# A gathered prefix sum and product: the last list chunk in a place of its own, merged front transfers, reordered transposes, four product groups

## The chip, the cores and the metric

The kernel runs on one core of one Trainium2 chip. The metric is the device time of one launch in microseconds: the median over runs of the same kernel, and for a comparison the two kernels are run in turn on one chip.

## The reference

```python
def reference(x, lengths, w):        # x 8 x 8192 x 512 f32, lengths 8, w 512 x 512 f32
    pos = np.arange(S)[None, :, None]
    mask = (pos < lengths[:, None, None]).astype(np.float32)
    cs = np.cumsum(x * mask, axis=1)
    midpoints = (lengths // 2).clip(0)
    mid_features = cs[np.arange(B), midpoints, :]
    return np.matmul(mid_features[:, None, :], w).squeeze(1)
```

Only one row of each running sum is used: the sum of the first `lengths // 2 + 1` rows of a batch. So the kernel sums those rows, batch by batch, and multiplies the eight sums by w. How many rows that is depends on the data in `lengths`. For the drawn lengths (1138, 5379, 511, 4113, 1809, 7542, 7716, 1140) some 31 MB have to be read.

## The kernel before

**Reading the rows.** A unit is U = 8 consecutive rows of one batch (16 KB). A chunk is 128 units, one on each partition (2 MB). There are three kinds of reads.

- The front: the first 256 rows of every batch are read blind, before the lengths are known, as two chunks into slots 0 and 1 of a ring `xt` of R = 4 slots. SP issues them (L149 to L153): chunk 0 (batches 0 to 3) as four transfers, each to every fourth partition; chunk 1 (batches 4 to 7) as one transfer to all partitions.
- The list: the units beyond the front that the lengths ask for are numbered through over all batches. DVE works out for every partition and chunk the unit's number (`idx`, mark "idx") and the 0/1 weights (`wc`, mark "w"). GpSimd (POOL) issues one indirect transfer a chunk (`gather(c)`, L234). Here the list has 1520 units, 11.875 chunks, so 12 gathers; units beyond the list are skipped by the bounds check. A gather waits until its slot is free: the first two for ACT's zeroing of slots 2 and 3 (`s_zero`, L185; skipped units must leave finite data), the others for PE's `s_done` of the chunk that held the slot.
- The back: rows 256 to 511 of batches 0 and 1 are again read blind, into `xb` (two transfers, 0.5 MB each). They and w (`wt`, one transfer for its first half and two for its quarters) stand at the end of POOL's queue (`gp_tail`, L251), behind the last gather.

**Summing.** PE multiplies each chunk's rows by its weights: 8 products of 128x8 by 128x512, in f32 with two passes each, spread over four groups of 32 output partitions (`add`, L395, with `u % 4`), so s_ps holds four partial sums of 8 rows each. Weights of a chunk go into the ring `wr`: ACT copies them from `wc` when a slot is free (`weigh`, L197). SP relays to PE that the weights and data of a chunk are there (`relay`, L167; semaphore `s_rdy`). Ahead of each chunk but the first, PE runs two filler products (`idle`, L418) that wait for nothing. SP, ACT and PE run their chunks in loops over the four slots (`ring`, L137) with a count in a register, since the number of chunks is data.

**The tail.** After the last chunk PE (block `pe_end`) multiplies the back piece of batch 0 (`back(0)`, L444) into c_ps, then (block `pe_last`) that of batch 1. DVE copies s_ps to s_sb in two halves once `s_done` has counted all chunks (L378). PE then folds and transposes: four products with s_sb's quarters as weights (L462) and one with c_sb (L465) give mf_ps, the sums with the feature dimension on the partitions. DVE copies it to mf_sb. Then w: for each of four k, two products of 128x8 by 128x256 into two groups of 64 output partitions (L469 to L475), with a wait for wt's piece at k = 0, 2, 3. DVE copies one half of the output from o_ps, ACT the other, and SP and ACT each store a half (8 KB).

**The order of work** is written out by hand, engine by engine; nothing schedules it. DVE's steps count up `s_dve`, and `marks` names the counts that others wait for. A DVE step waits for the one before unless it says `wait=False`. Each DMA queue takes its transfers in the order of issue: SP's holds the front, POOL's all gathers, xb and wt.

Of the kernel before, what the change touches and what calls it, by code (L numbers as in the profile page):

```python
# [15 lines left out]
def kernel(  # L16
# [30 lines left out]
    FAR = 1 << 17  # L47
    IDLE = 2
    xu = x.rearrange("b (q u) d -> (b q) (u d)", u=U)
    lens_words = lengths.tensor.reshape([B]).bitcast(I32).ap().rearrange("(o t) -> o t", o=1)  # L50

# [8 lines left out]
    def sem(name):  # L60
        return tc.alloc_semaphore(name)

    xt = sb("xt", [P, R, U * D])
    xb = sb("xb", [P, BB, BU * D])
    wt = sb("wt", [P, KC, D])
# [32 lines left out]
    ge = sb("ge", [P, C, B + 1])  # L98
    idx = sb("idx", [P, C], I32)
    early = sb("early", [P, C, U, B])  # L100
    wc = sb("wc", [P, C, U * B])
    wr = sb("wr", [P, R * U * B])
    wb = sb("wb", [P, BB, BU, BB])
    fold_i = sb("fold_i", [P, B], I32)
# [17 lines left out]
    s_full = [sem(f"full{k}") for k in range(R)]  # L122
    s_front = [sem(f"front{k}") for k in range(FRONT)]
    s_back = [sem(f"back{k}") for k in range(BB)]
    s_w = [sem(f"w{k}") for k in range(3)]
    s_len, s_out, s_pool, s_dve, s_pe, s_done, s_wr, s_rdy, s_zero, s_act = (
        sem(n) for n in ("len", "out", "pool", "dve", "pe", "done", "wr", "rdy", "zero", "act"))

# [19 lines left out]
    def sync(sp):  # L148
        for b in range(FB):  # L149
            sp.dma_start(out=xt[b::FB, 0], in_=x[b, :HEAD].rearrange("(q u) d -> q (u d)", u=U),  # L150
                         ).then_inc(s_front[0], 16)
        sp.dma_start(out=xt[:, 1], in_=x[FB:, :HEAD].rearrange("b (q u) d -> q b (u d)", u=U),
                     ).then_inc(s_front[1], 16)  # L153
        left = sp.alloc_register("left_sp")
        full = sp.alloc_register("full_sp")
        have = sp.alloc_register("have_sp")
        sp.reg_mov(full, 16)
        sp.reg_mov(have, 1)
        sp.wait_ge(s_dve, marks["chunks"])
        sp.load(left, chunks[:])  # L160
        sp.wait_ge(s_dve, marks["front"])
        for f in range(FRONT):
            sp.wait_ge(s_front[f], 16 if f else 16 * FB)
            sp.sem_inc(s_rdy, 1)
        sp.br(f"sy_0_{FRONT}")

        def relay(s):  # L167
            sp.wait_ge(s_wr, have)
            sp.wait_ge(s_full[s], full)
            sp.sem_inc(s_rdy, 1)  # L170
            sp.reg_add(have, have, 1)
            if s == FRONT - 1:
                sp.reg_add(full, full, 16)

        ring(sp, "sy", left, relay)
        with nc.body("sy_end", valid_engines=[sp.engine]):
            sp.wait_ge(s_dve, marks["out"])
            store(sp, 0)
            sp.wait_ge(s_out, 32)
            sp.br(END)  # L180


    def scalar(act):
        act.dma_start(out=lens[:], in_=lens_words).then_inc(s_len, 16)
        for s in range(FRONT, R):  # L185
            act.memzero(xt[:, s]).then_inc(s_zero, 1)  # L186
        left = act.alloc_register("left_act")
        free = act.alloc_register("free_act")
        act.wait_ge(s_dve, marks["w"])
        act.load(left, chunks[:])  # L190
        for s in range(FRONT, R):
            act.copy(out=weights_of(s), in_=wc[:, s - FRONT]).then_inc(s_wr, 1)  # L192
        act.reg_sub(left, left, R)
        act.reg_mov(free, 1)
        act.br("ac_0_0")

        def weigh(s):  # L197
            act.wait_ge(s_done, free)
            col = act.snap(free)
            act.copy(out=weights_of(s),  # L200
                     in_=wc[:, bass.ds(col + (R - FRONT - 1), 1)].rearrange("p c e -> p (c e)"),
                     ).then_inc(s_wr, 1)
            act.reg_add(free, free, 1)

        ring(act, "ac", left, weigh)
        with nc.body("ac_end", valid_engines=[act.engine]):
            act.wait_ge(s_pe, 5)
            act.copy(out=o_sb[64:64 + B], in_=o_ps[64:64 + B, :D // 2]).then_inc(s_act, 1)  # L208
            act.wait_ge(s_act, 1)
            store(act, 1)  # L210
            act.br(END)
# [5 lines left out]
    def gpsimd(pool):  # L217
        pool.iota(p_i[:], pattern=[[0, 1]], base=0, channel_multiplier=1).then_inc(s_pool, 1)
        pool.wait_ge(s_pool, 1)
        for k in range(4):  # L220
# [11 lines left out]
                  ).then_inc(s_pool, 1)  # L232

        def gather(c):  # L234
            s = (c + FRONT) % R
            if c < R - FRONT:
                pool.wait_ge(s_zero, c + 1)
            else:
                pool.wait_ge(s_done, c + FRONT - R + 1)
            pool.indirect_dma_start(  # L240
                out=xt[:, s], out_offset=None, in_=xu,
                in_offset=bass.IndirectOffsetOnAxis(ap=idx[:, c:c + 1], axis=0),
                bounds_check=B * UB - 1, oob_is_err=False,
            ).then_inc(s_full[s], 16)

        n = pool.alloc_register("n_pool")
        pool.wait_ge(s_dve, marks["idx"])
        gather(0)
        pool.load(n, count[:])
        pool.br("gp_1")  # L250
        with nc.body("gp_tail", valid_engines=[pool.engine]):  # L251
            for b in range(BB):
                pool.dma_start(out=xb[:, b], in_=x[b, BACK].rearrange("(q u) d -> q (u d)", u=BU),  # L253
                               ).then_inc(s_back[b], 16)
# [5 lines left out]
            pool.br(END)  # L260
        for c in range(1, C):
            with nc.body(f"gp_{c}", valid_engines=[pool.engine]):
                pool.br_cmp(n, c, f"gp_go{c}", "gp_tail", "IS_GT")  # L263
            with nc.body(f"gp_go{c}", valid_engines=[pool.engine]):
                gather(c)
                pool.br(f"gp_{c + 1}" if c + 1 < C else "gp_tail")

# [4 lines left out]
    def vector(dve):  # L272
# [48 lines left out]
        step(ts, out=count[:], in0=up_i[:], scalar1=7, scalar2=None, op0=ALU.logical_shift_right)  # L321
        step(ts, out=chunks[:], in0=count[:], scalar1=float(FRONT), scalar2=None, op0=ALU.add)
        mark("chunks")
# [29 lines left out]
        for f in range(FRONT):  # L353
# [10 lines left out]
             in1=ge[:, :, :B].unsqueeze(2).to_broadcast((P, C, U, B)), op=ALU.mult)  # L364
        mark("w")
        fill(pick[:], 0)
        fill(wb[:], 0)
# [7 lines left out]
        mark("back")  # L375
        left = dve.alloc_register("left_dve")
        dve.load(left, chunks[:])
        dve.wait_ge(s_done, left)  # L378
        for at in HALVES:
            step(dve.tensor_copy, out=s_sb[:, at], in_=s_ps[:, at])  # L380
        mark("s")
        dve.wait_ge(s_pe, 3)
        step(dve.tensor_copy, out=c_sb[:], in_=c_ps[:, :P])
        mark("c")
        dve.wait_ge(s_pe, 4)
        step(dve.tensor_copy, out=mf_sb[:].rearrange("p k m -> p (k m)"), in_=mf_ps[:])
        mark("mf")
        dve.wait_ge(s_pe, 5)
        step(dve.tensor_copy, out=o_sb[:B], in_=o_ps[:B, :D // 2])
        mark("out")  # L390
# [3 lines left out]
    def tensor(pe):  # L394
# [9 lines left out]
        with nc.body("pe_main", valid_engines=[pe.engine]):  # L404
            pe.reg_mov(begin, 0)
            pe.wait_ge(s_dve, marks["ones"])
            for to, width in ((s_ps, D), (o_ps, D // 2), (c_ps, P), (mf_ps, KC * B)):
                pe.matmul(to[:, :width], lhsT=zero[:, :P], rhs=zero[:, :width], start=True, stop=False,  # L408
                          skip_group_check=True)
# [8 lines left out]
        def idle():  # L418
            for _ in range(IDLE):
                pe.matmul(idle_ps[:FB], lhsT=v_f[:, 0], rhs=rank[:].to_broadcast((P, D)),  # L420
                          start=True, stop=True, skip_group_check=True)

        def chunk(s):
            pe.sem_inc(s_rdy, -1)._wait_ge(s_rdy, 1)  # L424
            for u in range(U):
                mm = add(s_ps, u % 4, weights_of(s)[:, u * B:(u + 1) * B],
                         xt[:, s, u * D:(u + 1) * D])
            mm.then_inc(s_done, 1)

# [11 lines left out]
        with nc.body("pe_end", valid_engines=[pe.engine]):  # L441
            pe.wait_ge(s_dve, marks["back"])

            def back(b):  # L444
# [12 lines left out]
        with nc.body("pe_last", valid_engines=[pe.engine]):  # L457
            back(1)
            for k, at in enumerate(QUARTERS):
                if k in (0, 2):  # L460
                    pe.wait_ge(s_dve, marks["s"] - 1 + k // 2)
                pe.matmul(mf_ps[:, B * k:B * (k + 1)], lhsT=s_sb[:, at], rhs=fold[:], start=False,  # L462
                          stop=False, skip_group_check=True)
# [5 lines left out]
            for k in range(KC):  # L469
                if k in W_AT:  # L470
                    pe.wait_ge(s_w[W_AT.index(k)], 16)
                for g, cols in enumerate(HALVES):
                    mm = pe.matmul(o_ps[64 * g:64 * g + B, :D // 2], lhsT=mf_sb[:, k],  # L473
                                   rhs=wt[:, k, cols], start=False, stop=(k == KC - 1),
                                   skip_group_check=True, tile_position=(0, 64 * g))  # L475
            mm.then_inc(s_pe, 1)
# [39 lines left out]
```

## Time and profile before

| | us |
|---|---|
| median of 14 runs (84.19 to 85.42) | 84.86 |
| the profiled execution | 84.48 |
| its span, first to last instruction | 82.7 |
| first bytes of the front in the trace | 2.2 |
| first chunk on PE, start | 10.03 |
| a list chunk, start to start (63.55 to 68.44) | 4.89 |
| last chunk's products on PE | 72.76 to 74.66 |
| landing of the second back piece | 75.16 |
| products with w on PE | 77.39 to 79.31 |

Busy time in the span: PE 59.9, of which 25.6 are filler, weight loads 16.2, DVE 13.5, ACT 11.6, POOL 16.8. The 16 DMA engines moved 31.25 MB: 27.00 MB on the queue of POOL, 4.20 MB on that of SP. The granted TensorE clock is 1.00 throughout. From the issue of a gather to its landing the median is 16.6 us; 18.0 to 18.4 us for wt.

How to read it: a group's line gives the source line, engine, operation, tiles with their shapes, the count and the busy time. PE's records come in pairs, PEld (weight load) and PE (the product), and an f32 product has two of each. All DVE steps have the line of a helper, L276, so they are told apart by their tiles; so do most products (L396). An end of a product is modelled. In a table of stretches each row gives the busy time of each engine in it, the clock, the DMA engines' mean busy share and the rate. Times are from the span's start.

### The profile page before, as it was taken

To read this page: it belongs to the slowest core of one execution; us is meant where nothing else is said; L and a number is where in the kernel's file an instruction comes from. 1 tells how busy PE (TensorE), PEld (TensorE's weight loads), DVE (VectorE), ACT (ScalarE), POOL (GpSimd) and SP (SyncE) were. 2 spreads that over 40 slices of the span, in tenths; PEclk is the share of its full clock that TensorE was granted. 3 is DMA by queue.
4 is the path that set the end of the run, shared out by engine and by line. 5 is a ranking of instruction groups with operands and counts; after the bars stand their busy time and mean duration, and the time that the engine had idled before them with its cause. 6 is when DMAs were issued, how large, how long until landed. Compare 5 with 4: busy or idle time off the path is not lost. (4 is left out here: it accounts for less than half of the span.)

```text
span 82.7 us, 1040 instructions
## 1 busy us (share of the span) xinstructions
PE 59.9 (72%) x346; PEld 16.2 (20%) x346; DVE 13.5 (16%) x55; ACT 11.6 (14%) x16; POOL 16.8 (20%) x33
## 2 busy tenths in 40 slices
PE   0980499999959498593958949396693948889830
PEld 0470211123112020110202112020211102026500
DVE  4718899600000000000000000000000000005010
ACT  2999700300101001010000101001000000000010
POOL 4400540504120404022040401307900000000000
PEclk9999999999999999999999999999999999999999
DMA  0999999999999999999999999999999999999000
GB/s 0 357 333 365 396 444 404 436 436 404 452 412 452 436 404 452 412 452 436 396 460 412 436 444 396 452 428 420 444 400 436 452 396 444 373 410 392 34 3 4
DMA packets 2693, 31.25 MB, mean 378 GB/s; under 512 B 386, under 2 KB 402, under 8 KB 914
## 3 DMA queue, kind: packets, MB, share of 16 engines
q0 software_dynamic: 2320, 27.00, 77.1%
q1 hardware_dynamic: 352, 4.20, 13.3%
q8 instruction: 1, 0.02, 0.1%
q14 instruction: 2, 0.02, 0.0%
q10 hardware_dynamic: 18, 0.01, 0.0%
HBM read 31.46 MB, written 0.02 MB: 381 GB/s over the span
## 5 line engine op out<-in xcount | busy, mean ns | idle before, releaser
L396 PE MATMUL s_ps<-xt,wr 128*8 128x512 f32 x224 | 29.1, 625 | 14.8 <-PEq L424 14.8
L420 PE MATMUL idle_ps<-rank,v_f 128*4 128x512 f32 x52 | 25.6, 615 | 0.0
L240 POOL DMA_INDIRECT xt<-in_x_dram,idx x12 | 12.2, 1020 | 42.0 <-PE s_ps L396 35.6
L396 PEld LDWEIGHTS s_ps<-xt,wr 128*8 128x8 f32 x224 | 5.7, 90 | 35.6 <-issue 35.5
L276 DVE COPY s_sb<-s_ps 128x256 f32<-128x256 f32 x2 | 0.8, 424 | 58.8 <-PE s_ps L396 58.7
L420 PEld LDWEIGHTS idle_ps<-rank,v_f 128*4 128x4 f32 x52 | 4.7, 90 | 19.0 <-issue 19.0
L200 ACT COPY wr<-wc 128x64 f32 x10 | 2.4, 244 | 38.1 <-PE s_ps L396 37.8
L186 ACT ACTIVATE xt<-xt 128x4096 uint32<-128x4096 uint32 x2 | 7.1, 3608 | 0.0
L208 ACT COPY o_sb<-o_ps 8x256 f32<-8x256 f32 x1 | 0.4, 362 | 23.1 <-PE o_ps L473 23.1
L408 PE MATMUL s_ps<-zero 1*128 1x512 f32 x2 | 2.0, 1122 | 1.9 <-DVE row L276 1.9
L412 PE MATMUL b_ps<-row,ones 1*128 1x16 f32 x2 | 0.6, 380 | 2.3 <-DVE row L276 2.3
L276 DVE TENSOR_TENSOR wc<-early,ge 128x1984 f32<-128x1984 f32 x1 | 2.2, 2224 | 0.0
L276 DVE TENSOR_TENSOR early<-v,b_ps 128x1984 f32<-128x1984 f32 x1 | 2.2, 2222 | 0.0
L473 PE MATMUL o_ps<-wt,mf_sb 128*8 128x256 f32 x16 | 1.9, 379 | 0.3 <-DVE mf_sb L276 0.3
L186 ACT ACT_TABLE_LOAD x1 | 1.3, 1283 | 1.5 <-SPq L52 1.5
L396 PE MATMUL c_ps<-xb,wb 128*2 128x128 f32 x32 | 1.3, 276 | 0.1
L253 POOL DMA_DIRECT2D xb<-in_x_dram x2 | 1.2, 594 | 0.0
L192 ACT COPY wr<-wc 128x64 f32<-128x64 f32 x2 | 0.4, 242 | 5.4 <-DVE wb L276 5.4
L258 POOL DMA_DIRECT2D wt<-in_w_dram x2 | 1.1, 594 | 0.0
L462 PE MATMUL mf_ps<-fold,s_sb 128*128 128x8 f32 x8 | 1.1, 262 | 0.0
L408 PE MATMUL o_ps<-zero 1*128 1x256 f32 x2 | 1.1, 629 | 0.0
L462 PEld LDWEIGHTS mf_ps<-fold,s_sb 128*128 128x128 f32 x8 | 1.0, 194 | 0.2 <-DVE s_sb L276 0.2
(67 smaller groups left out, 18.8 us busy)
## 6 DMA issues: line engine op xcount, KB each, us to landing
xt<-in_x_dram SPq DMA_DIRECT2D x4, 512.0 KB
xt<-in_x_dram SPq DMA_DIRECT2D x1, 2048.0 KB, 11.0
xb<-in_x_dram POOLq DMA_DIRECT2D x2, 512.0 KB, 16.9
wt<-in_w_dram POOLq DMA_DIRECT2D x1, 512.0 KB, 18.0
wt<-in_w_dram POOLq DMA_DIRECT2D x2, 256.0 KB, 18.3
xt<-in_x_dram,idx POOLq DMA_INDIRECT x12, 16.6
lens<-in_lengths_dram ACTq DMA_DIRECT2D x1, 0.1 KB
out_dram<-o_sb ACTq DMA_DIRECT2D x1, 8.0 KB
```

What stands on the lines that cost most here:

```text
L186: act.memzero(xt[:, s]).then_inc(s_zero, 1)
L200: act.copy(out=weights_of(s), in_=wc[:, bass.ds(col + (R - FRONT - 1), 1)].rearrange("p c e -> p (c e)"),).then_inc(s_wr, 1)
L240: pool.indirect_dma_start(out=xt[:, s], out_offset=None, in_=xu, in_offset=bass.IndirectOffsetOnAxis(ap=idx[:, c:c + 1], axis=0), bounds_c ...
L253: pool.dma_start(out=xb[:, b], in_=x[b, BACK].rearrange("(q u) d -> q (u d)", u=BU),).then_inc(s_back[b], 16)
L258: pool.dma_start(out=wt[:, k], in_=w[QUARTERS[k]]).then_inc(s_w[k - 1], 16)
L276: do(*args, **kw).then_inc(s_dve, 1)
L396: return pe.matmul(to[32 * j:32 * j + weights.shape[1], :rows.shape[1]], lhsT=weights, rhs=rows, start=False, stop=False, skip_group_check ...
L408: pe.matmul(to[:, :width], lhsT=zero[:, :P], rhs=zero[:, :width], start=True, stop=False, skip_group_check=True)
L412: pe.matmul(to[:, :of.shape[1]], lhsT=ones[:], rhs=of[:], start=True, stop=True,).then_inc(s_pe, 1)
L420: pe.matmul(idle_ps[:FB], lhsT=v_f[:, 0], rhs=rank[:].to_broadcast((P, D)), start=True, stop=True, skip_group_check=True)
L462: pe.matmul(mf_ps[:, B * k:B * (k + 1)], lhsT=s_sb[:, at], rhs=fold[:], start=False, stop=False, skip_group_check=True)
L473: mm = pe.matmul(o_ps[64 * g:64 * g + B, :D // 2], lhsT=mf_sb[:, k], rhs=wt[:, k, cols], start=False, stop=(k == KC - 1), skip_group_check ...
```

## The change

- **Front.** SP issues each front chunk as one transfer, chunk 0 in the form of chunk 1: partition 4q + b holds unit q of batch b.
- **Last list chunk.** The ring holds one list chunk fewer. The last has a place `xl` of its own, which ACT zeroes instead of slots 2 and 3, with its weights in `wl`. It is fetched by two indirect transfers of 128 pieces of 8 KB: half h holds the units' rows 4h to 4h + 3, numbered `2 * idx + h` by two new DVE steps. They go at the head of `gp_tail`, which no longer waits for a free slot; gathers 0 and 1 wait for no zeroing either. POOL loads the count ahead of gather 0 instead of behind it.
- **PE.** The last chunk stands in `pe_end`, without filler ahead of it; it waits for each half's own semaphore, and four products follow each.
- **Transposes.** `pe_last` runs the transposes of the first two quarters of s_sb, then the back piece of batch 1, then the other two.
- **Products with w.** Sixteen of 128x8 by 128x128 into four groups of 32 output partitions, in place of eight of 256 columns in two groups. DVE and ACT each copy two pieces of 8x128 to o_sb; DVE's second doesn't wait for its first.
- DVE's copy of s_ps waits for PE's count `s_pe` instead of the chunk count, and the later counts move up by one.

```diff
     def sync(sp):
-        for b in range(FB):
-            sp.dma_start(out=xt[b::FB, 0], in_=x[b, :HEAD].rearrange("(q u) d -> q (u d)", u=U),
-                         ).then_inc(s_front[0], 16)
-        sp.dma_start(out=xt[:, 1], in_=x[FB:, :HEAD].rearrange("b (q u) d -> q b (u d)", u=U),
-                     ).then_inc(s_front[1], 16)
+        for f in range(FRONT):
+            sp.dma_start(out=xt[:, f], in_=x[FB * f:FB * (f + 1), :HEAD].rearrange(
+                "b (q u) d -> q b (u d)", u=U)).then_inc(s_front[f], 16)
...
     def scalar(act):
-        for s in range(FRONT, R):
-            act.memzero(xt[:, s]).then_inc(s_zero, 1)
+        act.memzero(xl[:]).then_inc(s_zero, 1)
...
-        act.load(left, chunks[:])
+        act.load(left, count[:])
+        act.reg_sub(left, left, 1)
+        last = act.snap(left)
+        act.copy(out=wl[:], in_=wc[:, bass.ds(last, 1)].rearrange("p c e -> p (c e)"),
+                 ).then_inc(s_wl, 1)
+        act.reg_add(left, left, FRONT)
...
-            act.copy(out=o_sb[64:64 + B], in_=o_ps[64:64 + B, :D // 2]).then_inc(s_act, 1)
+            for j in range(2):
+                act.copy(out=o_sb[64:64 + B, j * P:(j + 1) * P],
+                         in_=o_ps[64 + 32 * j:64 + 32 * j + B, :P]).then_inc(s_act, 1)
...
         def gather(c):
             s = (c + FRONT) % R
-            if c < R - FRONT:
-                pool.wait_ge(s_zero, c + 1)
-            else:
+            if c >= R - FRONT:
                 pool.wait_ge(s_done, c + FRONT - R + 1)
...
         with nc.body("gp_tail", valid_engines=[pool.engine]):
+            pool.wait_ge(s_zero, 1)
+            pool.wait_ge(s_dve, marks["idx_h"])
+            for h in range(HALF):
+                fetch(xl[:, h], xh, idx_h[:, h:h + 1], B * S // UH, s_last[h])
...
     def vector(dve):
+        for h in range(HALF):
+            step(ts, out=idx_h[:, h:h + 1], in0=idx[:, bass.ds(at, 1)], scalar1=float(HALF),
+                 scalar2=float(h), op0=ALU.mult, op1=ALU.add)
+        mark("idx_h")
...
-        step(dve.tensor_copy, out=o_sb[:B], in_=o_ps[:B, :D // 2])
+        for j in range(2):
+            step(dve.tensor_copy, out=o_sb[:B, j * P:(j + 1) * P], in_=o_ps[32 * j:32 * j + B, :P],
+                 wait=False)
...
     def tensor(pe):
         with nc.body("pe_end", valid_engines=[pe.engine]):
             pe.wait_ge(s_dve, marks["back"])
+            pe.wait_ge(s_wl, 1)
+            for h in range(HALF):
+                pe.wait_ge(s_last[h], 16)
+                mm = slabs(wl[:, h * UH * B:(h + 1) * UH * B], xl[:, h], UH)
+            mm.then_inc(s_pe, 1)
...
         with nc.body("pe_last", valid_engines=[pe.engine]):
-            back(1)
             for k, at in enumerate(QUARTERS):
+                if k == 2:
+                    back(1)
                 if k in (0, 2):
                     pe.wait_ge(s_dve, marks["s"] - 1 + k // 2)
...
-                for g, cols in enumerate(HALVES):
-                    mm = pe.matmul(o_ps[64 * g:64 * g + B, :D // 2], lhsT=mf_sb[:, k],
-                                   rhs=wt[:, k, cols], start=False, stop=(k == KC - 1),
-                                   skip_group_check=True, tile_position=(0, 64 * g))
+                for j in range(4):
+                    mm = add(o_ps, j, mf_sb[:, k], wt[:, k, j * P:(j + 1) * P])
```

More of the change, by code (lines that the diff above doesn't have):

```diff
@@ L48 @@
     IDLE = 2
+    HALF = 2
+    UH = U // HALF
     xu = x.rearrange("b (q u) d -> (b q) (u d)", u=U)
+    xh = x.rearrange("b (q u) d -> (b q) (u d)", u=UH)
     lens_words = lengths.tensor.reshape([B]).bitcast(I32).ap().rearrange("(o t) -> o t", o=1)
@@ L63 @@
     xt = sb("xt", [P, R, U * D])
+    xl = sb("xl", [P, HALF, UH * D])
     xb = sb("xb", [P, BB, BU * D])
@@ L99 @@
     idx = sb("idx", [P, C], I32)
+    idx_h = sb("idx_h", [P, HALF], I32)
     early = sb("early", [P, C, U, B])
@@ L102 @@
     wr = sb("wr", [P, R * U * B])
+    wl = sb("wl", [P, U * B])
     wb = sb("wb", [P, BB, BU, BB])
@@ L123 @@
     s_front = [sem(f"front{k}") for k in range(FRONT)]
+    s_last = [sem(f"last{k}") for k in range(HALF)]
     s_back = [sem(f"back{k}") for k in range(BB)]
     s_w = [sem(f"w{k}") for k in range(3)]
-    s_len, s_out, s_pool, s_dve, s_pe, s_done, s_wr, s_rdy, s_zero, s_act = (
-        sem(n) for n in ("len", "out", "pool", "dve", "pe", "done", "wr", "rdy", "zero", "act"))
+    s_len, s_out, s_pool, s_dve, s_pe, s_done, s_wr, s_rdy, s_zero, s_act, s_wl = (
+        sem(n) for n in ("len", "out", "pool", "dve", "pe", "done", "wr", "rdy", "zero", "act", "wl"))
     END = "gather_end"
@@ L162, in sync @@
         for f in range(FRONT):
-            sp.wait_ge(s_front[f], 16 if f else 16 * FB)
+            sp.wait_ge(s_front[f], 16)
             sp.sem_inc(s_rdy, 1)
@@ L206, in scalar @@
         with nc.body("ac_end", valid_engines=[act.engine]):
-            act.wait_ge(s_pe, 5)
-            act.copy(out=o_sb[64:64 + B], in_=o_ps[64:64 + B, :D // 2]).then_inc(s_act, 1)
-            act.wait_ge(s_act, 1)
+            act.wait_ge(s_pe, 6)
+            for j in range(2):
+                act.copy(out=o_sb[64:64 + B, j * P:(j + 1) * P],
+                         in_=o_ps[64 + 32 * j:64 + 32 * j + B, :P]).then_inc(s_act, 1)
+            act.wait_ge(s_act, 2)
             store(act, 1)
@@ L232, in gpsimd, with fetch @@
                   ).then_inc(s_pool, 1)
+        def fetch(to, units, at, n, full):
+            pool.indirect_dma_start(
+                out=to, out_offset=None, in_=units,
+                in_offset=bass.IndirectOffsetOnAxis(ap=at, axis=0),
+                bounds_check=n - 1, oob_is_err=False).then_inc(full, 16)
         def gather(c):
             s = (c + FRONT) % R
-            if c < R - FRONT:
-                pool.wait_ge(s_zero, c + 1)
-            else:
+            if c >= R - FRONT:
                 pool.wait_ge(s_done, c + FRONT - R + 1)
[L240 to L244, printed above, removed]
+            fetch(xt[:, s], xu, idx[:, c:c + 1], B * UB, s_full[s])
         n = pool.alloc_register("n_pool")
         pool.wait_ge(s_dve, marks["idx"])
-        gather(0)
         pool.load(n, count[:])
-        pool.br("gp_1")
+        pool.br("gp_0_0")
         with nc.body("gp_tail", valid_engines=[pool.engine]):
+            pool.wait_ge(s_zero, 1)
+            pool.wait_ge(s_dve, marks["idx_h"])
+            for h in range(HALF):
+                fetch(xl[:, h], xh, idx_h[:, h:h + 1], B * S // UH, s_last[h])
             for b in range(BB):
@@ L260, in gpsimd @@
             pool.br(END)
[L261 to L264, printed above, removed]
+        for c in range(C - 1):
+            with nc.body(f"gp_0_{c}", valid_engines=[pool.engine]):
+                pool.br_cmp(n, c + 1, f"gp_1_{c}", "gp_tail", "IS_GT")
+            with nc.body(f"gp_1_{c}", valid_engines=[pool.engine]):
                 gather(c)
-                pool.br(f"gp_{c + 1}" if c + 1 < C else "gp_tail")
+                pool.br(f"gp_0_{c + 1}" if c + 2 < C else "gp_tail")
     marks = {}
@@ L321, in vector @@
         step(ts, out=count[:], in0=up_i[:], scalar1=7, scalar2=None, op0=ALU.logical_shift_right)
-        step(ts, out=chunks[:], in0=count[:], scalar1=float(FRONT), scalar2=None, op0=ALU.add)
+        step(ts, out=chunks[:], in0=count[:], scalar1=float(FRONT - 1), scalar2=None, op0=ALU.add)
         mark("chunks")
@@ L365, in vector @@
         mark("w")
+        at = dve.alloc_register("last_dve")
+        dve.load(at, count[:])
+        dve.reg_sub(at, at, 1)
+        at = dve.snap(at)
+        for h in range(HALF):
+            step(ts, out=idx_h[:, h:h + 1], in0=idx[:, bass.ds(at, 1)], scalar1=float(HALF),
+                 scalar2=float(h), op0=ALU.mult, op1=ALU.add)
+        mark("idx_h")
         fill(pick[:], 0)
@@ L375, in vector @@
         mark("back")
-        left = dve.alloc_register("left_dve")
-        dve.load(left, chunks[:])
-        dve.wait_ge(s_done, left)
+        dve.wait_ge(s_pe, 3)
         for at in HALVES:
@@ L381, in vector @@
         mark("s")
-        dve.wait_ge(s_pe, 3)
+        dve.wait_ge(s_pe, 4)
         step(dve.tensor_copy, out=c_sb[:], in_=c_ps[:, :P])
         mark("c")
-        dve.wait_ge(s_pe, 4)
+        dve.wait_ge(s_pe, 5)
         step(dve.tensor_copy, out=mf_sb[:].rearrange("p k m -> p (k m)"), in_=mf_ps[:])
         mark("mf")
-        dve.wait_ge(s_pe, 5)
-        step(dve.tensor_copy, out=o_sb[:B], in_=o_ps[:B, :D // 2])
+        dve.wait_ge(s_pe, 6)
+        for j in range(2):
+            step(dve.tensor_copy, out=o_sb[:B, j * P:(j + 1) * P], in_=o_ps[32 * j:32 * j + B, :P],
+                 wait=False)
         mark("out")
@@ L406, in tensor @@
             pe.wait_ge(s_dve, marks["ones"])
-            for to, width in ((s_ps, D), (o_ps, D // 2), (c_ps, P), (mf_ps, KC * B)):
+            for to, width in ((s_ps, D), (o_ps, P), (c_ps, P), (mf_ps, KC * B)):
                 pe.matmul(to[:, :width], lhsT=zero[:, :P], rhs=zero[:, :width], start=True, stop=False,
@@ L421, in idle, with slabs @@
                           start=True, stop=True, skip_group_check=True)
+        def slabs(weights, rows, n):
+            for u in range(n):
+                mm = add(s_ps, u % 4, weights[:, u * B:(u + 1) * B], rows[:, u * D:(u + 1) * D])
+            return mm
         def chunk(s):
             pe.sem_inc(s_rdy, -1)._wait_ge(s_rdy, 1)
[L425 to L428, printed above, removed]
+            slabs(weights_of(s), xt[:, s], U).then_inc(s_done, 1)
         for s in range(R):
```

## The prediction

> **What bounds the kernel now.** I read the 40-slice table first, then the chain that ended last, then rates by stretch, and last the timeline of the tail. The page's slices:
>
> ```profile
> PE   0980499999959498593958949396693948889830
> DMA  0999999999999999999999999999999999999000
> GB/s 0 357 333 365 396 444 404 436 436 404 452 412 452 436 404 452 412 452 436 396 460 412 436 444 396 452 428 420 444 400 436 452 396 444 373 410 392 34 3 4
> ```
>
> DMA is full from 2 to about 76.5 us; PE is padded with filler products (L420). So the transfer stream sets the time, and behind it hangs a tail of 6 us that moves almost no bytes. The chain of waits shows where the tail hangs:
>
> ```profile
> 57.87 17.29 DMA xb<-in_x_dram
> 75.16 0.04 issue
> 75.20 0.64 PE c_ps L396 x14
> 75.84 1.01 PE mf_ps L462 x8
> 76.86 0.26 PE mf_ps L465 x2
> ...
> 77.39 1.92 PE o_ps L473 x16
> 79.31 0.03 issue
> 79.33 0.41 DVE o_sb L276
> ```
>
> The second back piece (xb) lands 17.29 us after its issue at 57.87, at 75.16, and everything after it is serial. Gathers wait some 16 us in the queue, three to four deep, so no stretch is short of work. But the rate differs (columns: length, busy PE, PEld, DVE, ACT, POOL, PE clock, DMA share, GB/s):
>
> ```profile
> 2.20:8.00 5.80, 3.72 (x10) 2.37 (x9) 3.44 (x17) 5.79 (x3) 0.84 (x6) 1.00 1.03 359
> 7.80:9.80 2.00, 0.60 (x2) 0.50 (x2) 1.68 (x10) 2.00 (x1) 1.21 (x1) 1.00 1.02 401
> 20.00:40.00 20.00, 15.10 (x89) 3.17 (x85) 0.00 (x0) 0.98 (x4) 3.94 (x4) 1.00 1.01 432
> ```
>
> The first 2.08 MB, which are front chunk 0 in four transfers of 32 rows, run at 359 GB/s; what follows (front chunk 1, one transfer, a little of the first gather) at 401; gathers at 432. ACT's memzeros fill both of the first two stretches, so they don't explain the step from 359 to 401.
>
> **The change part by part.** The sum is made on the profiled execution: span 82.7, time 84.48, so 1.78 lies around the span; the median of the runs is 84.86. I carry the difference over to the median.
>
> *Front chunk 0 as one transfer.* SP issues two transfers instead of five (3.52 + 0.60 us before). Chunk 0 takes the form of chunk 1, so I cost it at chunk 1's row: 2.08/0.401 = 5.2 instead of 5.8, which is 0.6 less. Ends: 0 (the slow start is the stream's own), and -0.9 (2.08/0.432 = 4.8). [...] I take -0.4, part of 0.6, since the first issue alone is slow whatever its form. This passes whole to the end only because the queue stays full: front and two gathers (8.4 MB) feed it until 22 us, and the third gather is issued at 14.45.
>
> *No zeroing of ring slots; count loaded ahead of gather 0.* Gather 1 no longer waits 1.17 us for ACT; a register load and two branches go ahead of gather 0. Both lie under the front transfers, which last to 13 us and more. 0; without that cover the load would cost some tenths.
>
> *Last chunk in its own place, in halves.* On POOL's queue it now stands, with xb and wt behind it, right after gather 10, which is issued at 51.43. So they enter one chunk (4.9 us) earlier, but POOL issues one indirect transfer more (0.98 us). They stand in the same order behind a full queue: 0. Rows become 8 KB. The 16 KB rows run at 432 GB/s, 2.31 us/MB; the stretch from 72.2 to 76.2, mostly 4 KB rows of xb and wt, at 406, 2.46 us/MB. Three extra cuts per 16 KB cost 0.15 us/MB, so one extra cut over 1.84 MB costs about 0.1. Ends 0 and +0.3 (one more completion, and each half skips its empty rows: DMA share was 0.73 in 71–72 us, where the skipped rows of the last chunk lie). I take +0.1. SP's relay and the filler before the chunk go.
>
> *DVE and ACT steps for the indices and weights of the last chunk.* Two tensor_scalars of 0.15 to 0.17, one copy of 0.24 and register work, at 15 us. They delay fold, pick and the first ring weights by about a microsecond; the former are needed after 72 us, the latter at 19.3, so 0.
>
> *Last chunk's products.* Half 0 runs while half 1 is on its way; half 1 leaves 8 passes instead of 16, so s_ps ends about 0.85 earlier. That clears room ahead of xb's landing and shortens nothing by itself.
>
> *Transposes between the back pieces.* The timeline of the tail:
>
> ```profile
> 75.20 0.33 PEld L396 LDWEIGHTS c_ps<-xb,wb 128*2 128x2 f32 x16 [0.40 <-DMA xb<-in_x_dram]
> 75.77 0.99 PEld L462 LDWEIGHTS mf_ps<-fold,s_sb 128*128 128x128 f32 x8 [0.24 <-DVE s_sb L276]
> 76.11 0.29 DVE L276 COPY c_sb<-c_ps 128x128 f32<-128x128 f32 x1 [0.51 <-PE c_ps L396]
> 76.69 0.30 PEld L465 LDWEIGHTS mf_ps<-pick,c_sb 128*128 128x128 f32 x2
> 77.39 1.90 PE L473 MATMUL o_ps<-wt,mf_sb 128*8 128x256 f32 x16 [0.28 <-DVE mf_sb L276]
> ```
>
> Half of the transposes (0.5) moves ahead of the landing: PE is free from about 74.3, the first half of s_sb is there by then. Next late is the copy of c_sb, ending 76.40: the L465 product starts at 76.44 instead of 76.69. Gain 0.25 and not 0.5. The new wait for s_sb has back(1) queued behind it; by my times it passes 0.3 before that piece lands. [...]
>
> *Products in four groups.* The nearest row is c_ps: 16 passes of 128 columns in four groups last 0.64 from weight load to modelled end, 0.91 to the start of the copy that reads them; 27 ns a pass. 32 passes: 1.07 to 1.34, from 77.14: 78.2 to 78.5. Now wt is next late. Its transfers land 18.0 to 18.4 after issue; the last is issued at about 59.5, so it lands near 77.9. Before it had 0.9 in hand (needed at 78.8). The four products behind it are 8 passes, 0.43 to 0.70: 78.3 to 78.6. I take 78.5 against 79.31: -0.8, the 0.25 included (ends -0.7 and -1.0).
>
> *Output copies.* Two of 8x128 on each engine for one of 8x256 (0.41 and 0.36). c_sb's copy of 128 columns takes 0.29, so two back to back are 0.43 (overlapped) to 0.59: +0.1, ends 0 and +0.2.
>
> Sum: -0.4 + 0.1 - 0.8 + 0.1 = -1.0. Span 81.7, profiled 83.5, median 83.9. All low ends together give -1.9 (83.0), all high ends -0.2 (84.7).
>
> **The rivals.**
> *The stream is not shortened.* The front stays at 359 GB/s and the halves cost 0.3; only the tail gains: 84.86 - 0.8 + 0.1 + 0.3 = 84.5. For it: I can't separate form from start. Against: the 401 row. 0.17.
>
> [...] 0.12.
>
> *The four groups don't overlap.* The products stay at 1.9, only 0.25 of the tail is gained: 84.86 - 0.25 - 0.4 + 0.1 + 0.1 = 84.4. The c_ps row speaks against it. 0.06.
>
> **How the numbers follow.** The likeliest case has 0.65, at 83.9, its own range 83.0 to 84.7. A measurement can tell about 0.5%, 0.4 us, from no change: faster is below 84.4, slower above 85.3. Of the 0.65, 0.58 lies below 84.4; of the stream rival 0.06, of the last 0.03: faster 0.67. Slower is the cold clock and a little unforeseen, 0.14; the rest, 0.19, is the same. The range leaves out the cold case and the far low corner: 83.1 to 85.0.
>
> **What would show it.** Front: over 390 GB/s from 2.2 to 8 us. Landing of xb's second piece about 0.3 earlier, at 74.9. The product on c_sb starts right behind its copy, not behind transposes; the products' group 1.1 to 1.4 long, its last four behind the last wt landing. Half products of the last chunk near 1.0, not 1.9. Wrong would be: xb landing later than 75.2, the tail's passes at twice their length, or products that wait for wt beyond 78.2.

## The result and the profile after

The changed kernel's median is 83.40 us (83.10 to 84.49) against 84.89 for the kernel before in the runs beside it: a ratio of 0.9828, 95% interval 0.9800 to 0.9856, which is 1.46 us less (1.22 to 1.70). The forecast was 83.9, 1.0 less. Medians are taken over all executions of a kernel; ratios and intervals leave out those more than 1.5% above the kernel's fastest. The profiled execution took 83.37 with a span of 81.6; that of before took 84.48 and lay 0.4 under its kernel's median, so the two profiles differ by only 1.1.

The slices of the page after:

```profile
DMA  0999999999999999999999999999999999999200
GB/s 0 345 418 394 474 410 410 458 418 398 466 410 418 450 418 450 426 410 450 434 410 450 426 410 450 434 402 438 442 402 442 442 386 410 412 410 402 94 7 2
```

The first slices have risen (345, 418, 394 for 357, 333, 365), the middle is as before. The same stretches as before (columns as there):

```profile
2.20:8.00 5.80, 3.51 (x11) 2.36 (x11) 3.87 (x18) 4.19 (x2) 0.84 (x6) 1.00 1.00 401
7.80:9.80 2.00, 0.78 (x6) 0.63 (x10) 1.69 (x9) 0.00 (x0) 1.22 (x1) 1.00 0.94 401
20.00:40.00 20.00, 14.81 (x88) 3.01 (x84) 0.00 (x0) 0.98 (x4) 3.96 (x4) 1.00 1.00 428
```

The stretch of chunk 0 now runs at the 401 GB/s that the prediction read for chunk 1, where it had 359. The end of the chain that ended last:

```profile
55.47 19.51 DMA xb<-in_x_dram
74.98 0.04 issue
75.03 0.63 PE c_ps L418 x13
75.66 0.54 PE mf_ps L492 x4
76.20 0.31 PE mf_ps L495 x2
...
76.78 1.23 PE o_ps L418 x32
78.01 0.02 issue
78.04 0.28 DVE o_sb L290
```

xb's second piece is issued 2.4 earlier (55.47 for 57.87) and lands 0.18 earlier: the queue is full, and an earlier issue only waits longer (19.51 for 17.29). From the landing to the first product with w it is 1.80, before 2.23; the products take 1.23 for 1.92. The timeline shows the moved steps:

```profile
70.36 1.04 PE L418 MATMUL s_ps<-xl,wl 128*8 128x512 f32 x8 [0.26 <-DMA xl<-in_x_dram,idx_h]
72.47 1.04 PE L418 MATMUL s_ps<-xl,wl 128*8 128x512 f32 x8 [1.06 <-DMA xl<-in_x_dram,idx_h]
73.75 0.33 PEld L418 LDWEIGHTS c_ps<-xb,wb 128*2 128x2 f32 x16 [1.16 <-DMA xb<-in_x_dram]
74.31 0.64 PE L492 MATMUL mf_ps<-fold,s_sb 128*128 128x8 f32 x4
75.03 0.33 PEld L418 LDWEIGHTS c_ps<-xb,wb 128*2 128x2 f32 x16 [0.17 <-DMA xb<-in_x_dram]
75.75 0.29 DVE L290 COPY c_sb<-c_ps 128x128 f32<-128x128 f32 x1 [1.28 <-PE c_ps L418]
76.09 0.30 PEld L495 LDWEIGHTS mf_ps<-pick,c_sb 128*128 128x128 f32 x2
77.56 0.12 PEld L418 LDWEIGHTS o_ps<-wt,mf_sb 128*8 128x8 f32 x8 [0.23 <-DMA wt<-in_w_dram]
78.04 0.59 DVE L290 COPY o_sb<-o_ps 8x128 f32<-8x128 f32 x2 [1.31 <-PE o_ps L418]
```

Two transposes stand ahead of the second back piece, in a pause; the product on c_sb follows its copy; and at 77.56 the last products wait 0.23 for the last piece of wt, the new bound that was forecast. PE's passes in the tail have their usual length: 1.04 for each half of the last chunk, where the whole took 1.90 before, and 0.63 for the second back piece, before 0.64.

### The profile page after: what moved, and what is told of

The parts are those of the page before. It is cut to its first block, busy times and chain, and to the rows that moved or that the text cites. A ratio compares the mean times of both kernels' runs of the same rounds, so it can differ in the third digit from the quotient of the medians.

```text
span 81.6 us, 1063 instructions
## 1 busy us (share of the span) xinstructions
PE 57.0 (70%) x358; PEld 15.1 (18%) x358; DVE 13.8 (17%) x58; ACT 8.1 (10%) x16; POOL 17.9 (22%) x34
## 5 line engine op out<-in xcount | busy, mean ns | idle before, releaser
L418 PE MATMUL s_ps<-xt,wr 128*8 128x512 f32 x208 | 26.4, 628 | 14.8 <-PEq L451 14.8
L442 PE MATMUL idle_ps<-rank,v_f 128*4 128x512 f32 x48 | 22.9, 599 | 0.0
L246 POOL DMA_INDIRECT xt<-in_x_dram,idx x11 | 11.3, 1027 | 38.0 <-PE s_ps L418 32.2
L418 PEld LDWEIGHTS s_ps<-xt,wr 128*8 128x8 f32 x208 | 5.0, 90 | 34.5 <-issue 34.5
L190 ACT ACTIVATE xl<-xl 128x4096 uint32<-128x4096 uint32 x1 | 3.6, 3617 | 0.0
L218 ACT COPY o_sb<-o_ps 8x128 f32<-8x128 f32 x2 | 0.5, 256 | 26.9 <-PE o_ps L418 26.8
L418 PE MATMUL s_ps<-xl,wl 128*8 128x512 f32 x16 | 2.1, 594 | 1.3 <-DMA xl<-in_x_dram,idx_h 1.3
L246 POOL DMA_INDIRECT xl<-in_x_dram,idx_h x2 | 2.0, 991 | 0.6 <-issue 0.6
L418 PE MATMUL o_ps<-wt,mf_sb 128*8 128x128 f32 x32 | 1.2, 273 | 0.3 <-DVE mf_sb L290 0.3
```

Of the source, the lines that this page charges most:

```text
L190: act.memzero(xl[:]).then_inc(s_zero, 1)
L218: act.copy(out=o_sb[64:64 + B, j * P:(j + 1) * P], in_=o_ps[64 + 32 * j:64 + 32 * j + B, :P]).then_inc(s_act, 1)
L246: pool.indirect_dma_start(out=to, out_offset=None, in_=units, in_offset=bass.IndirectOffsetOnAxis(ap=at, axis=0), bounds_check=n - 1, oob_ ...
L418: return pe.matmul(to[32 * j:32 * j + weights.shape[1], :rows.shape[1]], lhsT=weights, rhs=rows, start=False, stop=False, skip_group_check ...
```

## The experiments

Times are medians; ratios are to the kernel before, run in turn with it on the same chip (its medians there were 84.94 to 85.03), with their 95% intervals.

**The front alone** (the kernel before with the diff's part in `sync`).

```diff
-        for b in range(FB):
-            sp.dma_start(out=xt[b::FB, 0], in_=x[b, :HEAD].rearrange("(q u) d -> q (u d)", u=U),
+        for f in range(FRONT):
+            sp.dma_start(out=xt[:, f], in_=x[FB * f:FB * (f + 1), :HEAD].rearrange(
+                "b (q u) d -> q b (u d)", u=U)).then_inc(s_front[f], 16)
```

> The kernel before with one part of the change: front chunk 0 in one transfer. [...] Zeroing (ACT's memzeros slow the transfers, and what helped in the changed kernel is that one of them went): below 370 GB/s, 84.9, no change.

84.15, ratio 0.9887 (0.9846 to 0.9928): 0.96 less. Its stretches, with ACT's two memzeros in place (5.79 and 2.00 busy):

```profile
2.20:8.00 5.80, 3.72 (x10) 2.37 (x9) 3.45 (x16) 5.79 (x3) 0.85 (x6) 1.00 1.00 401
7.80:9.80 2.00, 0.60 (x2) 0.49 (x2) 1.67 (x10) 2.00 (x1) 1.22 (x1) 1.00 0.98 418
```

So zeroing has no part in it. The gain is over twice the 0.4 that I took, and by the median just above the high end of 0.9 (the interval, 0.6 to 1.3, holds that end).

**The last chunk alone** (own place and halves, no zeroing of slots; front, transposes and products as before).

```diff
+            for h in range(HALF):
+                fetch(xl[:, h], xh, idx_h[:, h:h + 1], B * S // UH, s_last[h])
...
+                pe.wait_ge(s_last[h], 16)
+                mm = slabs(wl[:, h * UH * B:(h + 1) * UH * B], xl[:, h], UH)
```

> The kernel before with one part: the last list chunk in a place of its own and in halves, and no zeroing of ring slots. Front, order of transposes and products as before. As forecast: 0 to +0.3, 84.9 to 85.2, since nothing behind xb's landing gets shorter and the 8 KB rows cost a little. Zeroing theory: one memzero less frees the stream, -0.3 to -0.5, 84.4 to 84.6.

The 22 executions fall into two groups. Eleven took 84.61 to 85.82 at a mean granted clock of 0.993 to 1.000; their ratio is 1.0006 (0.9976 to 1.0036), as forecast: nothing. The other eleven took 86.35 to 87.30 at 0.964 to 0.980, so that the median of all is 86.09, 1.1 above the kernel before. That half was not forecast for this part.

**The order of the transposes alone.**

```diff
-            back(1)
             for k, at in enumerate(QUARTERS):
+                if k == 2:
+                    back(1)
```

> The kernel before with one part: the transposes of two quarters ahead of the second back piece. Without halves the first half of s_sb is copied at 75.14, just as xb lands at 75.16, so the second back piece queues behind 0.5 of transposes and the copy of c_sb comes later: +0.2 to +0.4, 85.1 to 85.3. If the order alone is worth its forecast -0.25: 84.65.

85.10, ratio 1.0007 (0.9974 to 1.0040): no gain, and not clearly the loss I expected. The mechanism is to be seen in the timeline:

```profile
74.97 0.88 DVE L276 COPY s_sb<-s_ps 128x256 f32<-128x256 f32 x2 [58.99 <-PE s_ps L396]
75.45 0.55 PEld L463 LDWEIGHTS mf_ps<-fold,s_sb 128*128 128x128 f32 x4 [0.39 <-DVE s_sb L276]
76.02 0.33 PEld L396 LDWEIGHTS c_ps<-xb,wb 128*2 128x2 f32 x16
76.75 0.29 DVE L276 COPY c_sb<-c_ps 128x128 f32<-128x128 f32 x1 [0.89 <-PE c_ps L396]
```

PE waits for s_sb, and the second back piece stands behind the transposes at 76.02 with no wait of its own: what the shorter stretch behind it saves is lost ahead of it.

**The products alone** (four groups, two output copies on each engine).

```diff
-                    mm = pe.matmul(o_ps[64 * g:64 * g + B, :D // 2], lhsT=mf_sb[:, k],
-                                   rhs=wt[:, k, cols], start=False, stop=(k == KC - 1),
+                for j in range(4):
+                    mm = add(o_ps, j, mf_sb[:, k], wt[:, k, j * P:(j + 1) * P])
```

> The kernel before with one part: the products with w in four groups, and the two output copies an engine. Passes at 27 ns: the group takes 1.1 to 1.3 instead of 1.92 and the copies 0.2 more, and the last piece of wt (77.9) comes in time: 84.2 to 84.4. If wt's landing holds it back: 84.5 to 84.7, with a gap ahead of the last four products.

84.30, ratio 0.9890 (0.9844 to 0.9935): 0.93 less. In its timeline:

```profile
78.06 1.06 PE L400 MATMUL o_ps<-wt,mf_sb 128*8 128x128 f32 x32 [0.28 <-DVE mf_sb L278]
79.19 0.54 ACT L209 COPY o_sb<-o_ps 8x128 f32<-8x128 f32 x2 [22.25 <-PE o_ps L400]
79.19 0.59 DVE L278 COPY o_sb<-o_ps 8x128 f32<-8x128 f32 x2 [1.18 <-PE o_ps L400]
```

1.06 for 1.90, with no wait for wt; the copies are 0.18 longer on each engine. That makes 0.66, inside the interval of the 0.93 (0.55 to 1.3). The whole times of the two profiled executions can't show it: this one took 84.50, since its second back piece starts on PE 0.69 later than in the profile of before (75.89 for 75.20).

**Four cut transfers.** Why does chunk 0 in four transfers lose? Front chunk 0 again in four, but each to all partitions.

```diff
-        for b in range(FB):
-            sp.dma_start(out=xt[b::FB, 0], in_=x[b, :HEAD].rearrange("(q u) d -> q (u d)", u=U),
+        for k in range(4):
+            cut = slice(k * U * D // 4, (k + 1) * U * D // 4)
+            sp.dma_start(out=xt[:, 0, cut], in_=x[:FB, :HEAD].rearrange(
+                "b (q u) d -> q b (u d)", u=U)[:, :, cut]).then_inc(s_front[0], 16)
```

> The kernel before, front chunk 0 still in four transfers, but each goes to all 128 partitions and is cut along the row (4 KB pieces). [...] Number of transfers (four short transfers with their completions cost the rate, whatever the partitions): 340 to 370 GB/s, 84.8 to 85.1.

The expectation missed: 85.56, ratio 1.0083 (1.0050 to 1.0116), and 294 GB/s over the whole slow stretch (297 from 2.2 to 9.6):

```profile
2.20:9.30 7.10, 4.32 (x12) 2.87 (x11) 4.56 (x22) 7.09 (x3) 1.81 (x7) 1.00 0.95 294
9.30:10.00 0.70, 0.00 (x0) 0.00 (x0) 0.57 (x4) 0.61 (x1) 0.24 (x1) 1.00 1.19 427
```

This run left two suspects beside the choice of partitions, the count of transfers and the size of the pieces. The next two runs have two transfers each; they vary the partitions, and the second also halves the cuts.

**Two transfers to 64 adjacent partitions each**, 16 KB pieces.

```diff
+        for j in range(2):
+            sp.dma_start(out=xt[64 * j:64 * j + 64, 0], in_=x[:FB, 128 * j:128 * j + 128].rearrange(
+                "b (q u) d -> q b (u d)", u=U)).then_inc(s_front[0], 16)
```

> The kernel before, front chunk 0 in two transfers of 64 adjacent partitions each, 16 KB pieces. [...] Number of transfers, whatever the partitions: between four (360 GB/s) and one (401), 84.2 to 84.7.

88.39, ratio 1.0432 (1.0371 to 1.0493). Half of the 429 to 432 GB/s that gathers reach, over more than 5 us:

```profile
2.00:5.00 3.00, 3.00 (x6) 1.75 (x7) 1.64 (x10) 2.99 (x2) 1.03 (x7) 1.00 1.09 262
5.00:10.00 5.00, 1.51 (x8) 1.29 (x6) 3.53 (x16) 4.91 (x2) 1.21 (x1) 1.00 0.99 210
```

The DMA engines' busy share is about 1 all the same (1.09 and 0.99): they are occupied, and each byte takes twice as long.

**Two transfers to all partitions**, cut along the row (8 KB pieces).

```diff
+        for k in range(2):
+            cut = slice(k * U * D // 2, (k + 1) * U * D // 2)
+            sp.dma_start(out=xt[:, 0, cut], in_=x[:FB, :HEAD].rearrange(
+                "b (q u) d -> q b (u d)", u=U)[:, :, cut]).then_inc(s_front[0], 16)
```

> The kernel before, front chunk 0 in two transfers over all partitions, cut along the row (8 KB pieces). If cutting the row is what slowed the four cut transfers (297 GB/s with 4 KB pieces): about 350 GB/s, 84.8 to 85.2. If the number of transfers did: about 380 to 400, 84.2 to 84.6.

84.07, ratio 0.9911 (0.9880 to 0.9942), 405 GB/s from 2.2 to 8.0: as good as one transfer. With the same count of transfers the partitions make 84.07 or 88.39; the pieces differ too, but the 16 KB of the slow form ran at 401 in one transfer to all partitions.

**The changed kernel with the front of before.**

> The changed kernel with the front of before. If the front's gain adds to the others, +0.8 to +1.0 over the changed kernel, 84.2 to 84.5. If another bound in the tail (wt's landing, PE) had taken part of it, only +0.3 to +0.5, 83.7 to 84.0.

84.30, ratio 0.9900 (0.9841 to 0.9958): by the ratios 0.6 more than the changed kernel, give or take half a microsecond. It can't tell the two expectations apart; most of the front's gain seems to arrive, but less than the front made alone (0.96).

**The last chunk whole, in its own place** (the changed kernel with `HALF = 1`).

> The changed kernel with the last list chunk in its own place but whole, in one transfer of 16 KB rows. If the halves matter as the room they make ahead of the second back piece: s_sb is late, the transposes push the back piece back, +0.2 to +0.4 over the changed kernel, 83.6 to 83.9. If only their cost counts (8 KB rows): -0.1, 83.3.

83.90, ratio 0.9874 (0.9816 to 0.9933): by the median 0.5 more than the changed kernel, but the intervals overlap (0.9800 to 0.9856 there), and two of the six executions, at 85.11 and 85.25, had a mean clock of 0.980 and 0.977. The timeline shows the mechanism:

```profile
72.63 1.90 PE L418 MATMUL s_ps<-xl,wl 128*8 128x512 f32 x16 [2.36 <-DMA xl<-in_x_dram,idx_h]
74.59 0.88 DVE L290 COPY s_sb<-s_ps 128x256 f32<-128x256 f32 x2 [58.63 <-PE s_ps L418]
75.07 0.55 PEld L492 LDWEIGHTS mf_ps<-fold,s_sb 128*128 128x128 f32 x4 [0.40 <-DVE s_sb L290]
75.64 0.33 PEld L418 LDWEIGHTS c_ps<-xb,wb 128*2 128x2 f32 x16
```

s_sb comes a microsecond later than with halves (74.59 for 73.58), the transposes start at 75.07 instead of 74.31, and the second back piece runs at 75.64 instead of 75.03. The halves are what lets the moved transposes run ahead of that piece.

**Filler between the halves**, on the last chunk alone and on the changed kernel.

```diff
+                if h == 0:
+                    idle(1)
```

> The kernel before with only the last chunk in its own place and in halves, as in the first set, plus one filler product behind the first half's products. Clock theory (PE rests between the halves, the clock is withdrawn for the tail in about half the executions, with mean clock near 0.978 and 1.6 us more): with the filler all executions lie at 84.5 to 85.5 and the mean clock at 0.99 to 1.00. If the two groups of times have another cause: still two groups, 85 and 87.

86.06, from 85.22 to 86.68; ratio 1.0136 (1.0073 to 1.0199), in which two of the four executions had a mean clock of 0.980. In all, four of six still had 0.967 to 0.980. The clock theory's expectation missed: one filler product there doesn't restore the clock. That PE's rest between the halves is what lowers it is not shown by any run.

> The changed kernel plus one filler product behind the first half's products. If PE's rest between the halves costs something in the median: 83.0 to 83.3. If not: 83.3 to 83.6, the same as the changed kernel.

83.19, ratio 0.9812 (0.9769 to 0.9856): not told apart from the changed kernel's 0.9828.

**Front and products, nothing else.**

> The kernel before with two parts of the change, the merged front and the four product groups; the last chunk stays in the ring and the transposes stay behind the second back piece. If the two gains (1.0 and 0.9) add: 83.0 to 83.3, and the last chunk's halves with the moved transposes are worth nothing. If the halves with the transposes are worth their 0.4: 83.5 to 83.9.

83.42, ratio 0.9833 (0.9792 to 0.9874), which is 1.42 less (1.07 to 1.77): by the medians the whole gain of the change. It lies between the two expectations, and below the 1.89 that the two parts made alone (0.96 + 0.93); the intervals are too wide to call that a loss. Its tail:

```profile
74.62 0.33 PEld L398 LDWEIGHTS c_ps<-xb,wb 128*2 128x2 f32 x16 [0.41 <-DMA xb<-in_x_dram]
76.81 0.77 PEld L398 LDWEIGHTS o_ps<-wt,mf_sb 128*8 128x8 f32 x32 [0.39 <-DVE mf_sb L276]
77.93 0.59 DVE L276 COPY o_sb<-o_ps 8x128 f32<-8x128 f32 x2 [1.18 <-PE o_ps L398]
```

From the start of the second back piece on PE to the products it needs 2.19, the changed kernel 1.75. But in this execution that piece starts at 74.62, in the changed kernel's at 75.03; and its products run through (1.06), while the changed kernel's wait for wt (1.19). So the copies start at 77.93 here and at 78.04 there.

## Why the prediction was right, and where its size was off

**The bound.** Right: a full stream and a tail behind it. Issuing earlier brought nothing, and the two parts that gained act on the stream's rate and on the tail.

**Front.** Right in that the form costs rate, and mis-sized: -0.4 was taken, -0.96 measured (0.6 to 1.3 less). The sum let the loss end with the stretch to 8.0, and then kept only part of its 0.6. The rest was left out because the first issue was held to be slow whatever its form. No run shows that: it took 1.64 with four transfers and 0.66 with one. The traces show that the loss goes on after 8.0:

```profile
2.20:9.60 7.40, 4.32 (x12) 2.87 (x11) 4.80 (x24) 7.39 (x3) 2.05 (x7) 1.00 1.01 361
2.20:9.60 7.40, 4.32 (x12) 2.86 (x11) 4.81 (x24) 7.39 (x3) 2.07 (x7) 1.00 1.02 414
```

The first row is the kernel before, the second the front alone. In the six profiled executions with the old front this stretch ran at 337 to 370 GB/s, in the five with the new one at 414 each. The bytes moved since 2.0, in MB:

| by | 4.0 | 8.0 | 9.6 | 20 | 70 |
|---|---|---|---|---|---|
| old front, mean of the six | 0.68 | 2.15 | 2.63 | 7.03 | 28.44 |
| new front, mean of the five | 0.63 | 2.34 | 3.06 | 7.45 | 28.86 |

The start is no faster with the new form (4.0). At 8.0 it leads by 0.2 MB, some 0.5 us at 428 GB/s, near the 0.6 of the sum; at 9.6 by 0.43. From 20 to 70 the lead stays at some 0.42 MB, 1.0 us, which is the measured gain: the full queue carries it to the end, as forecast. The second back piece starts on PE at 75.20 to 76.43 in five of the six and at 74.62 to 75.03 in four of the five; in the two others transposes hold it up.

The row of 401 was a weak base besides. The profile books a packet whole: in slices of 0.2 us the rates are multiples of 82 GB/s, one packet of 16 KB. Moved to 8.0 to 9.6, the same stretch of the kernel before reads 369.

Why the old form is slow is not shown. The choice of partitions can halve the rate: 64 adjacent partitions ran at 210 to 262, all partitions in as many transfers at 405. That every fourth partition loses by the choice of partitions too is the author's estimate. The count of four is a rival: four transfers to all partitions were slower still (294, in smaller pieces), and four with 16 KB pieces on better spread partitions were not tried. That the new form steps over batches 16 MiB apart costs nothing that shows here: they were read at 401 to 418.

**Zeroing.** Right, 0: the new front ran at 401 with both memzeros in place, and the last chunk alone, which drops one of them, gained nothing. Gather 0, with the count's load ahead of it, is issued at 8.51 for 8.33.

**Last chunk, halves and transposes.** Costed at +0.1 and -0.25. Each alone gave 0 (the last chunk in the eleven executions with the full clock); together, beside front and products, also 0 (83.40 and 83.42). Yet the transposes' share on PE was larger than -0.25: from the start of the second back piece to the products 1.75 for 2.19. The further 0.19 is c_sb's copy, which starts 0.72 after that piece for 0.91 before; that is not explained. Of the 0.44, 0.13 was lost again at wt, which was named as the next bound. The rest went with the later start of the back piece, 75.03 for 74.62; one execution of each can't say how much of that is the 8 KB rows. That the halves "shorten nothing by themselves" and make the room for the transposes agrees with the timeline of the whole chunk. One reading was wrong without effect: the transfers behind the last gather enter 2.4 earlier, and not 4.9 less 0.98, since the wait that goes is 3.92 and each further issue comes 0.3 after the one before.

**Products and copies.** Forecast 1.07 to 1.34, measured 1.06 without a wait and 1.19 with one; -0.8 + 0.1 covers them together with the transposes. Alone they gave -0.93, of which the trace accounts for 0.66. The copies don't overlap on DVE: 0.59 for two of 0.28, the upper end.

**The sum.** -1.0 against -1.46. The two profiled executions nearly meet it with -1.1: from the start of the second back piece on PE to the copies of the output 4.13 became 3.01, and the copies grew by 0.18, so the tail gave -0.94 (forecast -0.7); that piece starts 0.17 earlier (forecast 0.3). What did not carry over is the step from there to the medians: the profile of before lay 0.4 under its median and has the earliest second back piece of the five with the old front. With 0.94 for the tail, some 0.5 of the 1.46 is left for the stream, which agrees with the 0.6 that the old front costs in the changed kernel. So both terms were too small, and the transposes' 0.25, which show on PE, did not show in the median.

**The rivals.** The stream was shortened (414 GB/s for 361 from 2.2 to 9.6); the groups overlap (1.06 for 1.90). The 0.12, and with it most of the 0.14 for slower, stood for a cold clock: TensorE in the tail at the pace of the first chunk, 3.60 for 1.90. No run shows what makes the clock drop; the 0.12 was the author's estimate. The changed kernel's profile shows nothing of it in the tail (a granted clock of 1.00 from 70 to the end, 1.04 for each half of the last chunk), though one of its executions, at 84.49, had a mean of 0.966. What lowers the mean clock in half of the executions of the last chunk alone stays open: filler between the halves didn't cure it, and none of those executions was traced. A low mean by itself says little. In the profile of the products alone (0.985) the clock reads 1.00 from 70 to 80, and PE's last product ends at 79.12: there the low mean costs the tail nothing. In that of the two transfers to 64 partitions (0.974) it reads 0.97 from 20 to 70, and 1.00 from 2 to 20 and from 70 to 75. As an estimate from these figures, 0.03 of 50 us is 1.5 us of TensorE's time, which counts only where PE is waited for; the two groups of the last chunk alone lie 1.8 apart.

**Open.** Four transfers of 4 KB pieces to all partitions ran at 294 GB/s, two of 8 KB at 405. The choice of partitions doesn't explain that, since both went to all: the DMA share from 2 to 8 was 0.89 with the four and 0.99 with the two, so with the four the engines stood idle in part. Neither count nor size was varied alone.

## What to carry to other kernels

In a kernel that a full transfer queue bounds, look at the rate stretch by stretch, with the busy share beside it: a share of 1 at a low rate (here 0.99 at 210 GB/s) means that the pieces themselves move slowly, and the destination's partitions are the first suspect (here 405 GB/s to all, 210 to 262 to 64 adjacent ones). One or two transfers to all 128 partitions did best here (84.15 and 84.07). A form that runs elsewhere in the same trace at a better rate is a fair estimate, if the stretches are long against a packet and cover the whole loss. In a serial tail, before counting what a step saves, ask which landing comes next: here part of the 0.44 won on TensorE met a wait for the last weights. And ask where in its kernel's range the profiled execution lies before a difference is carried over to medians.

## What the runs showed of the hardware that I had not expected

- Two transfers to 64 adjacent partitions each: 210 to 262 GB/s at a busy share of 1.0 to 1.1, against 405 for two to all partitions.
- Four transfers of 4 KB pieces to all partitions: 294 GB/s, though the stretch of mostly 4 KB pieces on POOL's queue (xb and w, 72.2 to 76.2 in the kernel before) ran at 406.
- With a front in one or two transfers to all partitions the executions lie closer together: 83.92 to 84.42 in six of the front alone and 83.93 to 84.48 in nine of the two cut transfers, 84.35 to 85.99 in sixteen of the kernel before.
- The first of four front transfers takes 1.64 to issue in the kernel before, the first of two to all partitions 0.66 in the changed kernel.
- The copy of c_sb starts 0.71 to 0.73 after the weight load of the second back piece where transposes or a wait of 0.95 stand between the two pieces, and 0.90 or 0.91 where the second follows the first after 0.40; not explained.
